# Two borrowed PSUM banks for the second pair behind a head, and its ScalarE work behind the first pair's third sum

## The chip, the cores and the metric

The kernel runs on one core of a Trainium2 chip. The core has TensorE (PE, the matmuls, with its weight loads PEld), VectorE (DVE), ScalarE (ACT), GpSimd (POOL) and SyncE (SP, which issues the loads). They run side by side and wait for each other by semaphores; each takes its own instructions in the order in which they stand. Matmuls write to PSUM; the other memory is SBUF. The metric is the device time of one execution in microseconds, the median of three runs: 1868.45 us (1867.77 to 1869.39).

## The reference

A two-layer encoder works on a prompt of 256 tokens and a sample of 512, in float32. Each layer has a mixer (an mLSTM in layer 0, windowed attention in layer 1) and a feed-forward part, each behind an RMS norm with a modulation and a residual. The change touches the feed-forward part alone:

```python
def conv_ffn(h, w_up, conv_w, conv_b, w_down):
    u = h @ w_up
    u = lax.conv_general_dilated(u, conv_w[:, None, :], window_strides=(1,),
                                 padding=((CONV_WIDTH // 2, CONV_WIDTH // 2),),
                                 dimension_numbers=('NWC', 'WIO', 'NWC'),
                                 feature_group_count=2 * D_FF) + conv_b
    g = u[..., :D_FF]
    val = u[..., D_FF:]
    return (jax.nn.silu(g) * val) @ w_down
```

The width of the model is 1024, that of g and of val 2816 each, and the conv has three taps.

## The kernel before

The two sequences stand side by side as 768 columns, features on the 128 partitions. A float32 product is made of three matmuls: a value is split into a high part (`whi`, a ScalarE CAST, line 236) and the rest (`wlo`, a DVE subtraction, line 237), and high x high, high x low and low x high are summed in PSUM.

The up projection runs in 11 rounds p; round p makes 256 features of g and 256 of val. Each is one *pair* (i = 0 and 1): two rows of 128 features. A pair isn't multiplied out directly. The 2x2 blocks of weights and activations are combined first, so that seven block products do instead of eight. The combined activations (`T1` to `T4`, `B11`, `B21`, `B22`, held as `zh`/`zl`, `yh`/`yl` and `bq`) are made once per layer; the combined weights are made for each pair from two loads of 512 KB (`raw`) by four POOL instructions (lines 1158, 1161, 1162, 1170), then split. One block product is 12 matmuls of 384 columns (lines 1125, 1126, 1128).

Round 0 is the *head*: its order on PE, ACT and DVE is written out by hand, and it also does, for round 1, the products with B11 and B21. So the two pairs of round 1 have `rest` set and five products each, which `pair` puts into banks e, b and d: T1 into e; T2 into b, which begins as a copy of what the head left (line 1174); then d begins as a copy of b (line 1185), and T3 is added to it, the *third sum*, which ScalarE copies out as u3 (line 1196); B22 is added to b; T4 is added to d, the *fourth sum*. DVE makes two rows from b plus e's copy (lines 1179, 1198) and from e plus u3 (line 1199); ScalarE evicts r2 (line 1138).

There are eight PSUM banks. Four are fixed in this part (`bank(0)` to `bank(3)`, named ps in the profile); four rotate (`pa`), and the down projection takes one of them for each of its tiles. A row that is done goes through the conv (ACT line 1356, DVE taps in lines 1358 and 1359), silu (1366), POOL's product of g and val (1371) and its split (236, 237); then `down` multiplies and DVE adds the residual (563).

Apart from the head a scheduler sets the order within each engine, from its own estimate of times. `issue_after(x)` holds instructions behind x on x's engine; `behind` are two instructions of the head. A *mark* is a matmul whose result is not used: it opens a bank for sums that don't begin with a fresh product, since the copy writes over it.

Of the kernel before, what the change touches and what calls it, by code (L numbers as in the profile page):

```python
# [25 lines left out]
H = T // 2  # L26
# [52 lines left out]
def col(t):  # L79

    return t + (GAP if t >= 256 else 0)
# [64 lines left out]
class Net:  # L146
# [1003 lines left out]
    def pair(self, pool, u, bank, rows, rest=False, behind=None):  # L1150


        nc = self.nc
        r1, r2 = rows
        rb, ra = (self.load(u, h) for h in (1, 0))
        q = [t[:, 512 * i : 512 * (i + 1)] for t in (ra, rb) for i in range(2)]
        tt = nc.gpsimd.tensor_tensor
        tt(q[2], q[2], q[3], ALU.add)
        if not rest:
            wa = self.split(ra)  # L1160
        tt(q[0], q[2], q[0], ALU.subtract)  # L1161
        tt(q[1], q[1], q[0], ALU.subtract)
        s1h, s1l = (pool.tile([P, 512], R, tag=t, name=self.nm(t), bufs=1) for t in ("s1h", "s1l"))
        part = lambda w, i: [t[:, 512 * i : 512 * (i + 1)] for t in w]
        fork = r1[:, col(H) :]
        if not rest:
            fork = a = bank(0)
            self.quarters(a, part(wa, 0), self.B11, True)
        self.fp_copy_split(s1h, s1l, q[2])
        tt(q[2], q[3], q[0], ALU.subtract)  # L1170
        wc = self.split(ra)
        wb = self.split(rb)
        e, b = bank(1), bank(2)
        nc.scalar.copy(b, fork)
        p5 = self.tmp([P, H])

        def fifth():
            self.quarters(e, (s1h, s1l), self.T1, True)
            nc.scalar.copy(p5, e)

        if not rest:
            fifth()
        self.quarters(b, part(wc, 0), self.T2, False)
        d = bank(3)
        fork = nc.scalar.copy(d, b)
        if behind:
            with self.tc.issue_after(fork.ins):
                behind()
        if rest:
            fifth()  # L1190
        else:
            self.quarters(a, part(wa, 1), self.B21, False)
            self.evict(r1, a)
        self.quarters(d, part(wb, 0), self.T3, False)
        u3 = self.tmp([P, H])
        nc.scalar.copy(u3, d)  # L1196
        self.quarters(b, part(wc, 1), self.B22, False)
        nc.vector.tensor_tensor(r1[:, col(H) :], b, p5, ALU.add)  # L1198
        nc.vector.tensor_tensor(r2[:, col(H) :], e, u3, ALU.add)
        self.quarters(d, part(wb, 1), self.T4, False)  # L1200
        self.evict(r2, d)

    def prepare(self, u0, l):

        flat = [z.rearrange("p j k t -> p (j k t)") for z in (self.zh, self.zl)]
        place = lambda j: [z[:, j : j + 1024] for z in flat]

        ahead = [place(12 * H), place(4 * H)]
        wa = place(0)
        spare = None  # L1210
        if l:

            spare = self.slab([P, 3072], R)
            wa = [spare[:, 1024 * (z + 1) : 1024 * (z + 2)] for z in range(2)]
        self.fp_copy_split(*wa, self.load(u0 + 1, 0))
        for i in range(0 if l else 2):
            self.fp_copy_split(*ahead[i], self.load(u0 + 3 + i, 0))
        return wa, ahead, spare
# [122 lines left out]
    def ffn(self, l, xt, pool, last_tile, apply, keep=None):  # L1341
        nc = self.nc
        u0 = U_FFN + l * NPART * 3
        early = self.prepare(u0, l)
        next(last_tile)

        urows = [self.slab([P, 4, TG]) for _ in range(2)]
        for urow in urows:
            nc.gpsimd.memset(urow[:, :, 256 : 256 + GAP], 0.0)

        behind = []

        def conv(u, y, ch):
            cb = self.cst(CB + l * 44 + ch)
            w = lambda tap: self.cst(CW + (l * 44 + ch) * 3 + tap)
            nc.scalar.activation(y, u, AF.Identity, bias=cb, scale=w(1))  # L1356
            stt = nc.vector.scalar_tensor_tensor
            stt(y[:, 1:], u[:, :-1], w(0), y[:, 1:], ALU.mult, ALU.add)  # L1358
            stt(y[:, :-1], u[:, 1:], w(2), y[:, :-1], ALU.mult, ALU.add)  # L1359


        held = []

        def silu(yrow):
            for j in range(2):
                nc.scalar.activation(yrow[:, j], yrow[:, j], AF.Silu)

        def product(yrow, g):
            for j in range(2):
                y = yrow[:, 2 + j]  # L1370
                nc.gpsimd.tensor_tensor(y, y, yrow[:, j], ALU.mult)  # L1371
                self.fp_copy_split(g[:, 0, j], g[:, 1, j], y)

        def up(p):
            urow = urows[0] if p == 0 else urows[1]
            fixed = lambda i: self.bank[i][:, :H]
            if p == 0:
                eng = mybir.EngineType
                self.ready(HALVES[0])
                with self.tc.manual_schedule(engines={eng.PE, eng.Activation, eng.DVE}):  # L1380
                    behind[:] = self.head(u0, last_tile, pool, urows, mark, early)
            yrow = self.slab([P, 4, TG])
            g = self.slab([P, 2, 2, TG], R)
            for i in range(2):
                if p:
                    rows = [urow[:, 2 * i + j] for j in range(2)]
                    with ExitStack() as order:
                        for ins in behind[2 * i :] if p == 1 else ():
                            order.enter_context(self.tc.issue_after(ins))

                        other = p == i == 1
                        bank = lambda j: self.pa()[:, :H] if j == 1 and other else fixed(j)
                        self.pair(pool, u0 + 3 * p + i, bank, rows, p == 1, held.pop() if held else None)
                for j in range(2):
                    conv(urow[:, 2 * i + j], yrow[:, 2 * i + j], i * FC + 2 * p + j)
                if i == 0:
                    held.append(lambda: silu(yrow))
            if p:
                product(yrow, g)
            else:  # L1400
                gate = held.pop()
                held.append(lambda: (gate(), product(yrow, g)))
            return g

        def mark(t):

            hi, _ = self.quarter(self.B11)
            self.mm(t, hi[0][:, :P], hi[0], True, True)

        def down(p, g):  # L1410
            ws = (w for _, w in self.halves(u0 + 3 * p + 2))
            chunk = lambda w, i: [t[:, 512 * i : 512 * (i + 1)] for t in w]

            def tile(w, c, rng):
                s0, s1, _ = rng
                o = self.pa()[:, : s1 - s0]
                cs = slice(c % 4 * P, (c % 4 + 1) * P)
                for i in range(2):
                    wh, wl = chunk(w, i)
                    gh, gl = (g[:, z, i, col(s0) : col(s0) + s1 - s0] for z in range(2))  # L1420
                    self.mm(o, wh[:, cs], gh, i == 0, False)
                    self.mm(o, wh[:, cs], gl, False, False)
                    self.mm(o, wl[:, cs], gh, False, i == 1)
                self.resid(xt, o, l, 40, c, rng)

            if p < NPART - 1:
                for h, w in enumerate(ws):
                    for rng in SAMPLE, PROMPT:
                        for c in range(4 * h, 4 * h + 4):
                            tile(w, c, rng)  # L1430
                return
            ws = list(ws)
            for rng in RANGES:
                norm = Norm(self, xt, rng, apply, last=keep is None and rng is RANGES[-1], adds=None if keep is not None else nc.vector)
                for c in range(KC):
                    tile(ws[c // 4], c, rng)
                    norm.square(c)
                    if keep is not None or rng is not RANGES[-1] or c < 3:
                        self.tick(0.65)
                if keep is not None:  # L1440
                    self.save_x(xt, keep, rng)
                self.start(rng, norm.stages())

        prev = None
        for p in range(NPART):
            g = up(p)
            if prev is not None:
                down(*prev)
            prev = (p, g)
        down(*prev)  # L1450
# [180 lines left out]
```

## Time and profile before

| what | value |
|---|---|
| median of three runs | 1868.45 us |
| profiled execution | 1867.75 us, span 1865.8 us |
| TensorE granted clock, mean | 0.990 |
| PE busy, whole span | 1801.3 us of 1865.8 |
| DVE / ACT / POOL busy | 1393.3 / 903.8 / 488.1 us |
| round 1's pairs, layer 0 and layer 1 | from about 560 and from about 1366 us |

In a row of the profile stand line, engine, operation and tiles (written <- read). A wait is put down to what ended it last. A timeline row gives start and duration in us; an instruction's duration has a tail in which the next one has begun. Waits of PE cost time only where PE has no other work in its order, and PE takes its matmuls in order.

### The profile page before, as it was taken

Reading aid. Unit: us, or ns where it says so; the run is one execution under the profiler, and the core shown is the slowest. Engines: PE = TensorE matmul, PEld = TensorE weight load, DVE = VectorE, ACT = ScalarE, POOL = GpSimd, SP = SyncE. Lnnn points to the kernel's source line nnn. Section 1 sums busy time; section 2 is a strip of 40 time slices with the busy share of each in tenths; the row PEclk is TensorE's granted clock in tenths of the full one; section 3 lists DMA queues with packets and bytes.
Section 4 is the critical chain, followed back from the end, with each engine's and each line's share of the span. In section 5 each row is a group of like instructions: output and inputs, shape, how many; then the busy total and the mean of one; then the engine's idle time right before and its main releaser. Section 6 shows DMA issues by size and latency. Waiting matters only on the chain. (4 is left out here: it accounts for less than half of the span.)

```text
span 1865.8 us, 29038 instructions
## 1 busy us (share of the span) xinstructions
PE 1801.3 (97%) x11270; PEld 1660.2 (89%) x11270; DVE 1393.3 (75%) x2296; ACT 903.8 (48%) x1832; POOL 488.1 (26%) x387
## 2 busy tenths in 40 slices
PE   6999999999999999999999999989999999999997
PEld 3988877888998999999999898879989999999996
DVE  4765676876689877777777768875998778777877
ACT  4444434344456444444444556763575444444443
POOL 1101001022024333333331313330134333333322
PEclk9999999999999999999999999999999999999998
DMA  8343546536312212222222321212222222222212
GB/s 328 119 151 120 181 159 226 191 109 209 114 40 79 80 59 69 70 70 72 69 70 82 102 91 41 86 59 91 80 80 80 68 68 69 68 68 68 68 35 68
DMA packets 64245, 184.48 MB, mean 99 GB/s; under 512 B 6167, under 2 KB 23831, under 8 KB 64108
## 3 DMA queue, kind: packets, MB, share of 16 engines
q1 hardware_dynamic: 64108, 182.63, 29.5%
q8 instruction: 88, 1.44, 0.3%
q14 instruction: 49, 0.40, 0.1%
HBM read 176.17 MB, written 6.43 MB: 98 GB/s over the span
## 5 line engine op out<-in xcount | busy, mean ns | idle before, releaser
L236 ACT CAST whi<-raw 128x1024 fp32r<-128x1024 f32 x237 | 248.4, 1048 | 368.7 <-PE pa L230 162.6
L237 DVE TENSOR_TENSOR wlo<-raw,whi 128x1024 fp32r<-128x1024 f32 x237 | 321.4, 1356 | 113.0 <-ACT whi L236 111.4
L230 PE MATMUL pa<-slab,whi 128*128 128x256 f32 (+1 forms) x1472 | 347.1, 332 | 3.3 <-DVE slab L563 3.3
L230 PEld LDWEIGHTS pa<-slab,whi 128*128 128x128 f32 x1472 | 254.0, 189 | 27.6 <-DVE slab L563 4.8
L563 DVE SCALAR_TENSOR_TENSOR slab<-pa,mod,slab 128x256 f32<-128x256 f32 (+1 forms) x368 | 211.6, 593 | 72.7 <-PE pa L230 72.3
L230 PE MATMUL ps<-zh,whi 128*128 128x256 f32 (+2 forms) x688 | 232.4, 339 | 6.5 <-ACT whi L236 5.2
L230 PE MATMUL pa<-slab,wlo 128*128 128x256 f32 (+1 forms) x736 | 234.5, 330 | 0.0
L230 PE MATMUL ps<-zh,wlo 128*128 128x256 f32 (+2 forms) x688 | 227.3, 333 | 2.6 <-DVE wlo L237 2.6
L230 PE MATMUL ps<-zl,whi 128*128 128x256 f32 (+2 forms) x688 | 227.5, 333 | 0.4 <-DVE zl L526 0.4
L1125 PE MATMUL ps<-zh,whi 128*128 128x384 f32 x504 | 172.3, 342 | 3.7 <-ACT nt L1196 1.9
L1126 PE MATMUL ps<-zl,whi 128*128 128x384 f32 x504 | 169.9, 337 | 0.8 <-DVE zl L1082 0.8
L1128 PE MATMUL ps<-zh,wlo 128*128 128x384 f32 x504 | 169.0, 335 | 0.0
L230 PEld LDWEIGHTS pa<-slab,wlo 128*128 128x128 f32 x736 | 139.3, 189 | 13.0 <-DVE wlo L237 0.4
L230 PEld LDWEIGHTS ps<-zh,whi 128*128 128x128 f32 x688 | 131.8, 192 | 18.8 <-ACT whi L236 6.3
L230 PEld LDWEIGHTS ps<-zh,wlo 128*128 128x128 f32 x688 | 131.5, 191 | 13.3 <-DVE wlo L237 3.6
L230 PEld LDWEIGHTS ps<-zl,whi 128*128 128x128 f32 x688 | 131.9, 192 | 9.5 <-DVE zl L526 0.8
L1161 POOL TENSOR_TENSOR raw<-raw,raw 128x512 f32<-128x512 f32 x40 | 52.0, 1301 | 320.0 <-DVE wlo L237 246.4
L1371 POOL TENSOR_TENSOR slab<-slab 128x772 f32<-128x772 f32 x44 | 86.4, 1965 | 169.4 <-DVE slab L1359 157.5
L1358 DVE SCALAR_TENSOR_TENSOR slab<-slab,cstt,slab 128x771 f32<-128x771 f32 x88 | 107.6, 1225 | 26.5 <-ACT slab L1356 26.4
L482 DVE SCALAR_TENSOR_TENSOR ada<-raw,silc,ada 128x1024 f32<-128x1024 f32 x84 | 106.7, 1306 | 11.0 <-DMA raw<-in_adaln_w_dram 11.0
L1359 DVE SCALAR_TENSOR_TENSOR slab<-slab,cstt,slab 128x771 f32<-128x771 f32 x88 | 110.7, 1258 | 0.8
L1356 ACT ACTIVATE slab<-slab,cstt 128x772 f32<-128x772 f32 x88 | 91.0, 1034 | 39.1 <-DVE slab L1198 36.1
(301 smaller groups left out, 4130.6 us busy)
## 6 DMA issues: line engine op xcount, KB each, us to landing
raw<-in_w_dram SPq DMA_DIRECT2D x208, 512.0 KB, 3.7
raw<-in_adaln_w_dram SPq DMA_DIRECT2D x84, 512.0 KB, 4.6
slab<-in_x_dram SPq DMA_DIRECT2D x12, 512.0 KB, 7.5
slab<-in_adaln_w_dram SPq DMA_DIRECT2D x12, 512.0 KB, 10.2
slab<-mrows SPq DMA_DIRECT2D x8, 384.0 KB, 6.2
xs<-slab SPq DMA_DIRECT2D x6, 512.0 KB, 3.1
bt<-brow SPq DMA_DIRECT2D x16, 192.0 KB, 3.1
slab<-xs SPq DMA_DIRECT2D x6, 512.0 KB, 6.0
```

The lines of the kernel that those rows point to most:

```text
L230: self.nc.tensor.matmul(out, lhsT, rhs, start=start, stop=stop)
L236: nc.scalar.copy(hi, src)
L237: return nc.vector.tensor_tensor(lo, src, hi.bitcast(F32), ALU.subtract)
L482: stt(acc[:, s], row, w, acc[:, s], ALU.mult, ALU.add)
L563: self.nc.vector.scalar_tensor_tensor(x, o, self.mod[l][:, gc + c, q : q + 1], x, ALU.mult, ALU.add)
L1125: mm(o, wh[:, k], hi[k], start=start and k == 0, stop=False, skip_group_check=True)
L1126: mm(o, wh[:, k], lo[k], start=False, stop=False, skip_group_check=True)
L1128: mm(o, wl[:, k], hi[k], start=False, stop=k == 3, skip_group_check=True)
L1356: nc.scalar.activation(y, u, AF.Identity, bias=cb, scale=w(1))
L1358: stt(y[:, 1:], u[:, :-1], w(0), y[:, 1:], ALU.mult, ALU.add)
L1359: stt(y[:, :-1], u[:, 1:], w(2), y[:, :-1], ALU.mult, ALU.add)
L1371: nc.gpsimd.tensor_tensor(y, y, yrow[:, j], ALU.mult)
```

## The change

Before, of the second pair of round 1 only e lay in a rotating bank. Now e and b do, both asked for ahead of the pair, and b's bank is opened by a mark. And `pair` returns the copy of its third sum; the second pair's instructions on ScalarE are held behind the first pair's copy. Lines from 1202 on are one higher after the change, those behind the new block in `up` five higher.

```diff
         u3 = self.tmp([P, H])
-        nc.scalar.copy(u3, d)
+        last = nc.scalar.copy(u3, d)
         self.quarters(b, part(wc, 1), self.B22, False)
...
         self.evict(r2, d)
+        return last.ins
...
                         for ins in behind[2 * i :] if p == 1 else ():
                             order.enter_context(self.tc.issue_after(ins))
-
-                        other = p == i == 1
-                        bank = lambda j: self.pa()[:, :H] if j == 1 and other else fixed(j)
-                        self.pair(pool, u0 + 3 * p + i, bank, rows, p == 1, held.pop() if held else None)
+                        bank = fixed
+                        if p == i == 1:
+
+                            others = {j: self.pa()[:, :H] for j in (1, 2)}
+                            mark(others[2])
+                            bank = lambda j: others.get(j) or fixed(j)
+                            order.enter_context(self.tc.issue_after(last))
+                        last = self.pair(pool, u0 + 3 * p + i, bank, rows, p == 1, held.pop() if held else None)
```

The order of the instructions moves at three places that matter, the same in both layers. First ScalarE, around the copy of the first pair's third sum. In the names, `nt_5647` is u3, `slab_5563` the conv's row with its silu, `whi_5695` and `whi_5699` the second pair's weights before, `s1h_5693` and `whi_5698` after. Before:

```order
L236 CAST whi_5695<-raw_5685 128x1024
L1138 COPY slab_5136<-pa_5385 128x128
L1138 COPY slab_5136<-pa_5385 128x256
L236 CAST slab_5564<-slab_5563 128x772
L1356 ACTIVATE slab_5563<-slab_5136,cstt 128x772
L1366 ACTIVATE slab_5563<-slab_5563 128x772
L236 CAST whi_5699<-raw_5683 128x1024
L1196 COPY nt_5647<-ps_4536 128x384
L1174 COPY ps_4535<-slab_5137 128x384
```

After:

```order
L1357 ACTIVATE slab_5563<-slab_5136,cstt 128x772
L236 CAST slab_5564<-slab_5563 128x772
L1367 ACTIVATE slab_5563<-slab_5563 128x772
L1196 COPY nt_5647<-ps_4536 128x384
L236 CAST s1h_5693<-raw_5686 128x512
L236 CAST whi_5698<-raw_5688 128x1024
L1174 COPY pa_5684<-slab_5137 128x384
```

The two CASTs ahead of the copy are gone from there, the second pair's casts now follow it, and the copy that begins the second pair's b goes into a rotating bank.

Then PE, where the first pair's fourth sum (`ps_4536`) and the second pair's T1 (`pa_5703` before, `pa_5683` after) meet. Before:

```order
L1125 MATMUL pa_5703<-zh,s1h_5690 128x384
L1126 MATMUL pa_5703<-zl,s1h_5690 128x384
L1128 MATMUL pa_5703<-zh,s1l_5691 128x384
L1125 MATMUL ps_4536<-zh,whi_5595 128x384
L1126 MATMUL ps_4536<-zl,whi_5595 128x384
L1128 MATMUL ps_4536<-zh,wlo_5596 128x384
```

After:

```order
L1125 MATMUL ps_4536<-zh,whi_5595 128x384
L1126 MATMUL ps_4536<-zl,whi_5595 128x384
L1128 MATMUL ps_4536<-zh,wlo_5596 128x384
L1125 MATMUL pa_5683<-zh,s1h_5693 128x384
L1126 MATMUL pa_5683<-zl,s1h_5693 128x384
L1128 MATMUL pa_5683<-zh,s1l_5694 128x384
```

T1 of the second pair stood between the third and the fourth sum; now it stands behind the fourth.

Last DVE, from the last tap of the first pair's second row on. Before (`s1l_5942` belongs to the third pair):

```order
L1198 TENSOR_TENSOR slab_5137<-ps_4535,nt_5600 128x384
L237 TENSOR_TENSOR wlo_5700<-raw_5683,whi_5699 128x1024
L1359 SCALAR_TENSOR_TENSOR slab_5563<-slab_5136,cstt,slab_5563 128x771
L1199 TENSOR_TENSOR slab_5137<-ps_4534,nt_5647 128x384
L237 TENSOR_TENSOR s1l_5942<-raw_5930,s1h_5941 128x512
```

After (`s1l_5694` and `wlo_5699` belong to the second pair, `wlo_5703` to its third sum):

```order
L1198 TENSOR_TENSOR slab_5137<-ps_4535,nt_5600 128x384
L237 TENSOR_TENSOR slab_5564<-slab_5563,slab_5564 128x772
L1360 SCALAR_TENSOR_TENSOR slab_5563<-slab_5136,cstt,slab_5563 128x771
L1199 TENSOR_TENSOR slab_5137<-ps_4534,nt_5647 128x384
L237 TENSOR_TENSOR s1l_5694<-raw_5686,s1h_5693 128x512
L237 TENSOR_TENSOR wlo_5699<-raw_5688,whi_5698 128x1024
L1359 SCALAR_TENSOR_TENSOR slab_5577<-slab_5137,cstt,slab_5577 128x771
L1360 SCALAR_TENSOR_TENSOR slab_5577<-slab_5137,cstt,slab_5577 128x771
L237 TENSOR_TENSOR slab_5564<-slab_5563,slab_5564 128x772
L1359 SCALAR_TENSOR_TENSOR slab_5577<-slab_5137,cstt,slab_5577 128x771
L237 TENSOR_TENSOR wlo_5703<-raw_5686,whi_5702 128x1024
```

The s1l behind that tap and L1199 is now the second pair's, and four conv and split instructions stand between its T2 weights and those of its third sum.

## The prediction

> **What bounds the kernel now.** First the page's head: TensorE's share says whether time can be won anywhere else.
>
> ```profile
> span 1865.8 us, 29038 instructions
> PE 1801.3 (97%) x11270; PEld 1660.2 (89%) x11270; DVE 1393.3 (75%) x2296; ACT 903.8 (48%) x1832; POOL 488.1 (26%) x387
> ```
>
> TensorE (PE) is idle for 65 us of 1865.8, and the change leaves its matmuls as they are but for two marks. So the change is worth what it does to PE's waits. Next, the table of waits of PE over the whole span (total, times, longest):
>
> ```profile
> PE ps L1128 <- DVE s1l L237: 2.8, 2, 1.4
> PE ps L1125 <- ACT nt L1196: 1.9, 2, 0.9
> PE ps L1125 <- ACT ps L1174: 1.4, 2, 0.7
> PE ps L1126 <- DVE bq L1107: 0.4, 2, 0.2
> PE pa L230 <- DVE slab L563: 3.3, 6, 0.7
> ```
>
> The first three come twice each, once behind the head of each layer, which is where the change is. Their places are in PE's timeline (start, duration; in brackets the idle time and who ended it):
>
> ```profile
> 567.39 0.34 PE L1125 MATMUL pa<-zh,s1h 128*128 128x384 f32 x1
> 567.58 0.34 PE L1126 MATMUL pa<-zl,s1h 128*128 128x384 f32 x1
> ...
> 573.55 0.34 PE L1128 MATMUL pa<-zh,s1l 128*128 128x384 f32 x1
> 574.81 0.44 PE L1125 MATMUL ps<-zh,whi 128*128 128x384 f32 x1 [0.93 <-ACT nt L1196]
> ...
> 576.84 0.34 PE L1128 MATMUL ps<-zh,wlo 128*128 128x384 f32 x1
> 577.88 0.44 PE L1125 MATMUL ps<-zh,whi 128*128 128x384 f32 x1 [0.70 <-ACT ps L1174]
> ...
> 580.25 0.34 PE L1126 MATMUL ps<-zl,s1h 128*128 128x384 f32 x1
> 581.97 0.45 PE L1128 MATMUL ps<-zh,s1l 128*128 128x384 f32 x1 [1.38 <-DVE s1l L237]
> ```
>
> In a run without waits a 384-column matmul starts 0.175 us after the one before, and the first after a wait loses 0.10 more. So the stops cost 1.26-0.18+0.10 = 1.18, 1.04-0.18+0.10 = 0.96 and 1.72-0.18+0.10 = 1.64: 3.78 us a layer, 7.6 in all. Behind this place little is left to win:
>
> ```profile
> 567.00:584.00 17.00, 13.99 (x77) 12.98 (x76) 16.96 (x14) 12.36 (x20) 10.47 (x5) 1.00 0.30 94
> 592.00:680.00 88.00, 87.80 (x505) 83.69 (x504) 68.55 (x79) 42.18 (x66) 32.95 (x20) 1.00 0.20 66
> ```
>
> In these stages (PE, PEld, DVE, ACT, POOL busy) PE is full from 592 on, so what is lost or won at 567 to 592 stays. In the stops themselves the full engine is VectorE (DVE), 16.96 of 17.00 us. Why it is full stands in its timeline beside GpSimd's (POOL):
>
> ```profile
> 568.40 2.50 POOL L1371 TENSOR_TENSOR slab<-slab 128x772 f32<-128x772 f32 x1 [5.97 <-ACT slab L1366]
> 570.87 2.01 POOL L1170 TENSOR_TENSOR raw<-raw,raw 128x512 f32<-128x512 f32 x1
> 579.52 1.84 POOL L1371 TENSOR_TENSOR slab<-slab 128x772 f32<-128x772 f32 x1 [4.43 <-DVE slab L1359]
> ```
>
> ```profile
> 566.43 1.21 DVE L237 TENSOR_TENSOR wlo<-raw,whi 128x1024 fp32r<-128x1024 f32 x1
> 567.57 0.68 DVE L237 TENSOR_TENSOR s1l<-raw,s1h 128x512 fp32r<-128x512 f32 x1
> 568.17 1.01 DVE L1358 SCALAR_TENSOR_TENSOR slab<-slab,cstt,slab 128x771 f32<-128x771 f32 x1
> 569.22 2.51 DVE L1359 SCALAR_TENSOR_TENSOR slab<-slab,cstt,slab 128x771 f32<-128x771 f32 x1
> 571.65 2.31 DVE L237 TENSOR_TENSOR wlo<-raw,whi 128x1024 fp32r<-128x1024 f32 x1
> 579.30 0.54 DVE L1199 TENSOR_TENSOR slab<-ps,nt 128x384 f32<-128x384 f32 x1
> 579.77 2.14 DVE L237 TENSOR_TENSOR s1l<-raw,s1h 128x512 fp32r<-128x512 f32 x1
> 585.93 0.95 DVE L237 TENSOR_TENSOR slab<-slab,slab 128x772 fp32r<-128x772 f32 x1
> ```
>
> DVE's instructions with two inputs in SBUF and POOL's take turns: the s1l split takes 0.68 at 567.57 and 2.14 at 579.77, where POOL's product began 0.25 earlier; the tap takes 1.01 at 568.17 and 2.51 at 569.22; the wlo split 1.21 and 2.31. A product thus holds DVE off for about 1.7, a POOL sum of 512 columns for 2.31-1.21 = 1.10. L1199, which reads one input from PSUM, takes its 0.54 beside a product.
>
> The Trainium skill, page "SBUF — State Buffer", section "Who interferes with whom", says the same as a rule: a VectorE instruction with two SBUF inputs and a GpSimd instruction that reads SBUF share a port pair, and whichever starts second waits for the other's whole instruction. By that rule the third stop would come back at whichever s1l follows the product; by the solo row, 0.68, it would not. The 2.14 agrees with the rule. With it the sum below is +3.4 us; with the solo rows it would be -4.2.
>
> **The change, part by part.** The second pair's work on ScalarE now stands behind the first pair's copy of its third sum (L1196), and its sums e and b lie in two banks of the other pool, so PE's order changes: third sum, fourth sum of the first pair with nothing between, then T1 and T2 of the second. I follow it through layer 0, by hand, with these rows (consecutive starts on DVE and ACT are 0.06 to 0.10 less than the durations: the wlo split occupies 1.14, a tap 0.93, the slab split 0.87, s1l 0.60).
>
> ```profile
> 567.47 0.85 ACT L1366 ACTIVATE slab<-slab 128x772 f32<-128x772 f32 x1
> 570.94 0.84 ACT L236 CAST slab<-slab 128x772 fp32r<-128x772 f32 x1 [1.25 <-POOL slab L1371]
> 573.36 1.03 ACT L236 CAST whi<-raw 128x1024 fp32r<-128x1024 f32 x1
> 574.29 0.47 ACT L1196 COPY nt<-ps 128x384 f32<-128x384 f32 x1
> ...
> 577.76 0.62 ACT L236 CAST s1h<-raw 128x512 fp32r<-128x512 f32 x1
> ```
>
> A load of half a weight unit takes, from issue to landing, among the loads of 550 to 600:
>
> ```profile
> DMA to landing us min/median/max: 3.5/3.6/3.7
> ```
>
> Removed: the three stops, -3.78. Added:
>
> *Stop A, third to fourth sum.* From 567.39 PE does 24 matmuls, 4.2 us, to 571.6. On DVE the s1l of 567.57 is gone, so wlo (to 567.57) is followed by a tap to 568.50. POOL's product, wanted from 568.2 (silu 567.3 to 568.15), holds to 570.13; the next tap ends at 571.06. The second silu waits for that tap: 571.2 to 571.95; the copy stands behind it: to 572.43. PE goes on at 572.47: 0.87+0.10 = 0.97. The floor, with ScalarE free, is one copy and two hand-overs, about 0.8; the whi CAST, 1.03 in the row above, is no longer ahead of it.
>
> *Stop B, s1l of the second pair.* Fourth sum to 574.57, two matmuls to 574.92. DVE from 571.06: tap 0.93; POOL's sum L1158 for the third pair, whose weights are asked for when wlo ends (567.6) and land 3.6 later, gets in for 1.10 (L1198, from PSUM, beside it); slab split 0.87; tap 0.93, to 574.9. That tap releases the second product, which holds 1.8 with its hand-over while L1199 runs: 576.7. Then s1l 0.60, 577.38 with its tail. PE resumes at 577.42: 2.50+0.10 = 2.60. If the split won against the product it would be ready at 576.05, 1.25; if POOL's sum got in one tap earlier, 3.05. I take 2.60, since the same sequence (tap, product, L1199, s1l) stands at 579.30 to 579.77 above.
>
> *Stop C, first weights of the down projection.* 22 matmuls, 3.95 with the restart, to 581.37. POOL's L1170 waits for s1l, then for the wlo split (to 578.45), and ends at 579.7; two CASTs at 0.95 follow on ScalarE: 581.75. 0.42+0.10 = 0.52; between 0 and 1.0, as a CAST more or less stands ahead.
>
> *Stop D, wlo of the second pair's third sum.* PE reaches it at 583.52. DVE after 578.45: L1170's 1.10, three taps and a slab split 3.66, wlo 1.14: 584.35, PE 584.47: 0.95+0.10 = 1.05. ScalarE's copy L1185 that starts this third sum (done at 583.08) is just in time.
>
> Sum 0.97+2.60+0.52+1.05 = 5.14 against 3.78: **+1.35 a layer**. Through stop D the end is set by DVE's row (571.06 plus 13.3 us, 3.3 of it POOL's two sums and part of the product), so a smaller B only makes C and D larger.
>
> *Third pair.* Its third sum now follows T2's last matmul after four others, and the copy L1185 between them stands behind a CAST. Where such a copy is late today it costs this:
>
> ```profile
> 674.15 0.34 PE L1128 MATMUL ps<-yh,wlo 128*128 128x384 f32 x1
> 674.69 0.45 PE L1125 MATMUL ps<-zh,whi 128*128 128x384 f32 x1 [0.20 <-ACT ps L1185]
> ```
>
> 0.54-0.18 = 0.36; bounds 0 and 0.46. I take 0.35 a layer.
>
> *Marks.* One more matmul per layer ahead of 548, 0.18 each; it is hidden by the wait for L1107 there (0.2 idle each time in the table), and costs 0.18 if that cover goes.
>
> *Banks.* The down projection has two fewer banks until the second pair's last adds are done (588 to 589 by this reckoning); PE wants its third bank at 594. Nothing.
>
> *Ripples.* The norms after layer 0 and the attention are ordered a little differently. PE idles 3.9 and 6.8 us there:
>
> ```profile
> 1000.00:1062.00 62.00, 58.10 (x403) 54.49 (x403) 48.95 (x91) 28.75 (x57) 20.16 (x20) 0.97 0.35 112
> 1198.00:1262.00 64.00, 57.17 (x457) 48.70 (x456) 48.84 (x205) 45.46 (x145) 20.94 (x39) 0.95 0.21 65
> ```
>
> No step there is added; I take 0, with 1.5 either way.
>
> Two layers: 2 x (1.35+0.35) = **+3.4 us**. The profiled execution took 1867.75, its span and 1.95 around it; the median is 0.70 above, and I add the sum to the median: 1871.9.
>
> **The rivals.** *Faster: DVE and POOL don't meet.* If stop B's s1l and D's wlo ran at their solo lengths (0.68, 1.21), only A and half of C are left, about 1.7 a layer against 3.78: -4.2, 1864.3. It decides if DVE's row ends about 2 us before 584.35 or more. For it: ScalarE gets to the copy earlier and loses the CAST ahead of it. Against it: 2.14 and 2.31 in the rows above.
>
> *The stops only change places.* New ones of 3.8 a layer, no third-pair wait: 1868.4. For it: the removed and added stops are alike in kind. It needs POOL's sum L1158 to fall wholly beside an instruction from PSUM, and stop C to vanish.
>
> *Slower: DVE stays behind into the down projection.* Then residual adds (L563) come late and PE finds its four banks unread, up to 0.7 a time by the wait table. Two or three more such waits a layer are 2.8 to 4.2 in all: 1874.7 to 1876. It decides if DVE is more than about 4 us later than I have it at 588. For it: DVE's 16.96 of 17.00. Against it: 68.55 of 88.00 just behind.
>
> **How the numbers follow.** About 0.2% (3.7 us) is what a measurement of this kernel tells from no change: 1864.7 to 1872.2. The forecast, 1871.9 (its own range 1870.0 to 1873.5), has 0.45 and lies across that bound: 0.25 within, 0.20 beyond. Stops that change places 0.13, DVE behind 0.30, no meeting 0.12. So faster 0.12, same 0.38, slower 0.50. From 1866.5 to 1876.0 leaves out nearly all of the faster case and a tail above, under 2 in 10.
>
> **What would show it.** The waits for L1174 and the first L1196 gone or moved: the fourth sum right behind the third with about 0.7 idle for L1196; an s1l wait of 2 to 2.5 us five to six us earlier than now, the split itself over 2 us long beside a product; shorter new waits for a whi CAST and a wlo split at 581 to 585; PE past the second pair's B22 at 588.4. An s1l of 0.68 there, or PE past it before 586, makes me wrong towards faster; waits for L563 after 594, towards slower.

## The result

The changed kernel takes 1872.09 us in the median of 13 executions (1867.3 to 1875.34), the kernel before 1868.11 in 13 executions beside them (1866.13 to 1870.7). The ratio is 1.0022, with a 95% interval of 1.0014 to 1.003: slower by about 4 us.

Its profiled execution has a span of 1872.7 us. Of the 6.9 us by which that is longer than the span shown of before, 3.3 were there already at 560 us, ahead of the place of the change: the first conv instruction of ScalarE in layer 0 stands at 561.96 instead of 558.65. So the two traces are compared by place. That distance, 3.31 ahead of the place, is 5.42 behind it (the same instructions at 756.06 and 761.48), 4.38 ahead of layer 1's, and 6.8 behind that: 2.1 and 2.4 us a layer, less 1.0 us in the attention between them, where no step was changed (the account of the prediction below shows that this 1.0 is not the change's).

The head of the page and the table of PE's waits of the changed kernel:

```profile
span 1872.7 us, 29033 instructions
PE 1806.8 (96%) x11272; PEld 1663.7 (89%) x11272; DVE 1392.0 (74%) x2296; ACT 904.5 (48%) x1832; POOL 485.4 (26%) x387
```

```profile
PE pa L1128 <- DVE s1l L237: 4.7, 2, 2.4
PE pa L230 <- DVE slab L563: 3.8, 8, 0.6
PE ps L1125 <- ACT nt L1196: 1.3, 2, 0.7
...
PE ps L1125 <- ACT ps L1185: 0.4, 2, 0.2
```

The wait for L1174 is gone, that for L1196 is shorter, that for s1l has grown from 1.4 to 2.4 each (before the change PE waited for the third pair's s1l, now for the second pair's), and two waits for L563 have come. PE's timeline of layer 0, from the end of the first pair's third sum to the second pair's:

```profile
574.73 0.34 PE L1128 MATMUL ps<-zh,wlo 128*128 128x384 f32 x1
575.72 0.44 PE L1125 MATMUL ps<-zh,whi 128*128 128x384 f32 x1 [0.65 <-ACT nt L1196]
...
578.11 0.34 PE L1126 MATMUL pa<-zl,s1h 128*128 128x384 f32 x1
580.82 0.45 PE L1128 MATMUL pa<-zh,s1l 128*128 128x384 f32 x1 [2.37 <-DVE s1l L237]
...
582.60 0.53 PE L1128 MATMUL pa<-zh,s1l 128*128 128x384 f32 x1
582.92 0.53 PE L1125 MATMUL pa<-zh,whi 128*128 128x384 f32 x1
...
585.80 0.34 PE L1125 MATMUL pa<-zh,whi 128*128 128x384 f32 x1
...
587.78 0.34 PE L1126 MATMUL ps<-zl,whi 128*128 128x384 f32 x1
587.95 0.39 PE L1128 MATMUL ps<-zh,wlo 128*128 128x384 f32 x1
```

Stop A is 0.99-0.18+0.10 = 0.91, stop B 2.71-0.18+0.10 = 2.63. Stops C and D are not there. In their place ten matmuls from 582.60 to 585.80 stand 0.32 apart instead of 0.176: 3.20 us for 1.76 us of work, 1.44 lost. The windows show why (the seventh number is the granted clock):

```profile
582.00:586.00 4.00, 4.00 (x16) 4.00 (x15) 3.96 (x4) 2.91 (x5) 1.04 (x1) 0.57 0.43 124
1388.00:1392.00 4.00, 3.81 (x14) 3.81 (x15) 3.96 (x4) 2.95 (x4) 2.19 (x1) 0.58 0.20 32
```

Half speed for some 3 us, in both layers. Before, this stretch ran at 1.00:

```profile
582.00:586.00 4.00, 4.00 (x20) 3.51 (x21) 4.00 (x4) 2.54 (x4) 1.94 (x1) 1.00 0.00 0
```

DVE and POOL meet as they did before, only earlier in PE's work:

```profile
577.25 1.01 DVE L1360 SCALAR_TENSOR_TENSOR slab<-slab,cstt,slab 128x771 f32<-128x771 f32 x1
578.18 0.55 DVE L1199 TENSOR_TENSOR slab<-ps,nt 128x384 f32<-128x384 f32 x1
578.64 2.12 DVE L237 TENSOR_TENSOR s1l<-raw,s1h 128x512 fp32r<-128x512 f32 x1
...
586.63 2.35 DVE L237 TENSOR_TENSOR wlo<-raw,whi 128x1024 fp32r<-128x1024 f32 x2
```

```profile
578.40 1.81 POOL L1372 TENSOR_TENSOR slab<-slab 128x772 f32<-128x772 f32 x1 [1.89 <-DVE slab L1360]
```

Further on, the down projection waits for a residual add, once a layer (607.21, and 0.55 idle at 1414.79), and the third pair for L1185 (the wait that was at 674.69 is gone):

```profile
607.21 0.73 PE L230 MATMUL pa<-slab,whi 128*128 128x512 f32 x2 [0.35 <-DVE slab L563]
618.85 0.44 PE L1125 MATMUL ps<-zh,whi 128*128 128x384 f32 x1 [0.18 <-ACT ps L1185]
```

### The profile page after: what moved, and what is told of

Read it like the earlier page. It is cut to its first block, busy times and chain, and to the rows that moved or that the text cites. A ratio compares the mean times of both kernels' runs of the same rounds, so it can differ in the third digit from the quotient of the medians.

```text
span 1872.7 us, 29033 instructions
## 1 busy us (share of the span) xinstructions
PE 1806.8 (96%) x11272; PEld 1663.7 (89%) x11272; DVE 1392.0 (74%) x2296; ACT 904.5 (48%) x1832; POOL 485.4 (26%) x387
## 3 DMA queue, kind: packets, MB, share of 16 engines
q8 instruction: 88, 1.44, 0.3%
## 4 chain that ended last, share of the span: by engine, by line
PE 78%; DVE 10%; issue 5%; DMA 3%; ACT 2%; POOL 1%; SPq 0%; POOLq 0%; DVEq 0%; ACTq 0%
PE ps L230 24%; PE pa L230 23%; PE ps L1125 10%; PE ps L1126 9%; PE ps L1128 9%; DVE wlo L237 1%; DMA raw<-in_w_dram 1%; DMA bt<-brow 1%; PE pa L965 1%; DVE slab L1359 1%; DMA raw<-in_adaln_w_dram 1%; DVE slab L563 1%; DVE slab L1360 1%; DVE t L941 1%; ACT whi L236 1%
## 5 line engine op out<-in xcount | busy, mean ns | idle before, releaser
L237 DVE TENSOR_TENSOR wlo<-raw,whi 128x1024 fp32r<-128x1024 f32 x237 | 316.2, 1335 | 118.5 <-ACT whi L236 115.6
L230 PE MATMUL pa<-slab,whi 128*128 128x256 f32 (+1 forms) x1472 | 346.7, 332 | 3.8 <-DVE slab L563 3.8
L230 PEld LDWEIGHTS pa<-slab,whi 128*128 128x128 f32 x1472 | 254.1, 189 | 28.3 <-DVE slab L563 5.9
L563 DVE SCALAR_TENSOR_TENSOR slab<-pa,mod,slab 128x256 f32<-128x256 f32 (+1 forms) x368 | 212.3, 593 | 75.6 <-PE pa L230 75.2
L230 PE MATMUL ps<-zh,whi 128*128 128x256 f32 (+2 forms) x688 | 233.3, 340 | 6.3 <-ACT whi L236 4.9
L230 PE MATMUL pa<-slab,wlo 128*128 128x256 f32 (+1 forms) x736 | 234.2, 330 | 0.0
L230 PE MATMUL ps<-zh,wlo 128*128 128x256 f32 (+2 forms) x688 | 227.7, 334 | 2.3 <-DVE wlo L237 2.3
L230 PE MATMUL ps<-zl,whi 128*128 128x256 f32 (+2 forms) x688 | 228.7, 334 | 0.7 <-DVE zl L526 0.7
L230 PEld LDWEIGHTS pa<-slab,wlo 128*128 128x128 f32 x736 | 139.3, 189 | 12.9
L230 PEld LDWEIGHTS ps<-zh,whi 128*128 128x128 f32 x688 | 132.6, 193 | 18.9 <-ACT whi L236 6.0
L230 PEld LDWEIGHTS ps<-zh,wlo 128*128 128x128 f32 x688 | 131.8, 192 | 12.8 <-DVE wlo L237 3.1
L230 PEld LDWEIGHTS ps<-zl,whi 128*128 128x128 f32 x688 | 132.6, 193 | 10.1 <-DVE zl L526 1.1
L1372 POOL TENSOR_TENSOR slab<-slab 128x772 f32<-128x772 f32 x44 | 82.2, 1869 | 166.7 <-DVE slab L1360 153.9
L1158 POOL TENSOR_TENSOR raw<-raw 128x512 f32<-128x512 f32 x40 | 65.6, 1640 | 187.7 <-DMA raw<-in_w_dram 170.8
```

The costliest lines, as they stand in the source:

```text
L230: self.nc.tensor.matmul(out, lhsT, rhs, start=start, stop=stop)
L237: return nc.vector.tensor_tensor(lo, src, hi.bitcast(F32), ALU.subtract)
L563: self.nc.vector.scalar_tensor_tensor(x, o, self.mod[l][:, gc + c, q : q + 1], x, ALU.mult, ALU.add)
```

## The experiments

Two readings of this stand against each other. *Theory*: DVE's row of instructions, with POOL's turns in it, sets when the stretch ends; the half clock only fills time in which PE would have waited at C and D. *Rival*: the half clock, 1.44 us a layer, is the loss, and without it the change would be about even. A second rival: the loan of the banks, or ScalarE's order, costs by itself. All ratios are to the kernel before, run beside each on the same chip.

| kernel | ratio | 95% interval |
|---|---|---|
| the change | 1.0022 | 1.0014 to 1.003 |
| the change again | 1.0021 | 1.0009 to 1.0032 |
| only the banks | 1.0020 | 1.0011 to 1.003 |
| only the order | 1.0028 | 1.0019 to 1.0038 |
| 12 unused matmuls | 1.0023 | 1.0014 to 1.0032 |
| product on DVE | 0.9999 | 0.9988 to 1.001 |
| early s1 split | 1.0048 | 1.003 to 1.0065 |
| early s1 split, product on DVE | 1.0015 | 1.0006 to 1.0023 |
| only the banks, product on DVE | 1.0001 | 0.999 to 1.0011 |
| before, product on DVE | 1.0001 | 0.9988 to 1.0015 |
| before, product on DVE, again | 0.9992 | 0.9982 to 1.0001 |

**One half of the change at a time.** Only the banks, without the hold behind L1196:

```diff
-                            order.enter_context(self.tc.issue_after(last))
```

> Only the two banks; the hold behind the copy of the third sum (L1196) is left out, so T1 and T2 of the second pair may stand between the first pair's third and fourth sum. Theory (the end of the stretch is set by DVE's and POOL's turns): PE then has 22 matmuls to do where it stopped 0.9 and 0.6 us in the trace of before, so those two stops go (-2.1 us a layer), but it arrives that much earlier at the s1l split behind the second POOL product, and the wait there grows from 1.4 to between 3 and 4 us: the stretch ends within 0.5 us a layer of before, 1867 to 1870. If the clock falls to half behind that longer stop, as it did in the trace of after, up to 1.4 us a layer more, 1871. Rival (banks and ScalarE's order are what cost or win): the s1l wait stays at 1.4, the two stops are won outright, -2.1 us a layer, 1864.

Only the hold, with the second pair's b in its fixed bank as before the change:

```diff
-                            others = {j: self.pa()[:, :H] for j in (1, 2)}
-                            mark(others[2])
+                            others = {1: self.pa()[:, :H]}
```

> Only the hold behind L1196; the second pair's b stays in its fixed bank, as before the change. Theory: PE's waits as in the trace of after (about 0.7 for L1196, 2.3 to 2.4 for s1l, a half clock behind it), span within 1 us of after, ratio to before 1.0015 to 1.0025; the banks alone cost nothing, unless the waits for the down projection's residual adds (L563, 0.4 and 0.6 in after) go with them, which would be -0.9 in all. Rival (the loan of a bank is what costs): the L563 waits go and the time is that of before.

Measured: 1873.05 with the banks, 1875.25 with the order, 1868.89 before. Each half alone costs about what both together cost, so they don't add up. With the banks alone, PE's timeline has this:

```profile
580.30 0.42 PE L1125 MATMUL ps<-zh,s1h 128*128 128x384 f32 x1 [1.91 <-DVE slab L1199]
580.56 0.34 PE L1126 MATMUL ps<-zl,s1h 128*128 128x384 f32 x1
582.26 0.46 PE L1128 MATMUL ps<-zh,s1l 128*128 128x384 f32 x1 [1.36 <-DVE s1l L237]
```

The stops for L1196 and L1174 are gone, PE has its 22 matmuls early, and then stands, in the third pair's T1, for 1.91 + 1.36 = 3.3 us: the wait foreseen for s1l, shared with L1199, which stands just ahead of it on DVE and frees the bank. Behind it the clock falls to 0.57 here too:

```profile
582.00:586.00 4.00, 3.74 (x12) 3.65 (x13) 3.96 (x5) 3.97 (x7) 1.69 (x1) 0.57 0.00 0
```

The 2.1 us a layer that the two stops had cost were not won. With the order alone PE waits 0.65 and 2.37 as in the changed kernel, and the waits for L563 (0.34 and 1.31) did not go. So the loss needs neither the loan nor the mark, and with the banks alone it does not need the hold: either half brings PE to DVE's late splits. The ratio with the order alone, 1.0028, lies a little above theory's 1.0015 to 1.0025: here PE comes to the wlo matmul of the third sum at 585.62 without a wait, 0.6 us after that split was done on DVE (583.83 plus 1.21), so a part of the half clock is paid there.

**Work for PE in the stop.** 12, then 4 unused matmuls into the rotating bank of e behind the first pair's fourth sum, so that PE stops for less or hardly at all (in the code the pair also returns its last matmul):

```diff
+                            with self.tc.issue_after(last[1]):
+                                for _ in range(12):
+                                    mark(others[1])
```

> The changed kernel with 12 unused matmuls of 384 columns (the opening matmul of a bank, whose result is written over) added in each layer behind the first pair's fourth sum, so that PE works through most of the wait for the s1l split: 12 times 0.176 is 2.1 of its 2.4 us. Nothing else moves. Theory (DVE's row sets the end): the idle time falls to about 0.3, the clock stays at 1.00 at 582 to 586, and the waits that the half clock covered come out: about 0.5 for the whi CAST ahead of the first down weights and up to 1.0 for the wlo split of the second pair's third sum; the stretch ends within 0.4 us a layer of after, 1871 to 1872.5. Rival (the half clock is what makes the change slower): those waits stay away, each layer wins 1.4 us, 1869.

> The changed kernel with 4 unused matmuls a layer behind the first pair's fourth sum instead of 12, 0.7 us of work: the stop for s1l is about 1.7 idle. If the length of the stop is what halves the clock, it stays at 1.00 here as in the kernel before behind a stop of 1.4, and the waits for the whi CAST and the wlo split of the third sum are back (1.5 to 2 us together). The time from the third sum of the first pair to the first wlo matmul of the second pair's third sum is 13.2 us as with 0 and with 12 extra matmuls, since DVE's row sets it.

> The changed kernel once more, beside the next two on one chip. The s1l stop of 2.4 comes in both layers again; if the half clock behind it is set by the stop, it comes in both layers again too (0.57 to 0.58 of 4 us); if it was a chance of that execution, it is missing in one or both, and waits for a whi CAST (about 0.4) and a wlo split (about 1.4) are there instead. The ratio to before is 1.0014 to 1.003 either way.

With 12 matmuls, PE's timeline and the windows:

```profile
573.33 0.34 PE L1128 MATMUL ps<-zh,wlo 128*128 128x384 f32 x1
574.34 0.44 PE L1125 MATMUL ps<-zh,whi 128*128 128x384 f32 x1 [0.67 <-ACT nt L1196]
...
579.47 0.44 PE L1128 MATMUL pa<-zh,s1l 128*128 128x384 f32 x1 [0.32 <-DVE s1l L237]
...
583.24 0.33 PE L1128 MATMUL pa<-zh,s1l 128*128 128x384 f32 x1
583.78 0.51 PE L230 MATMUL pa<-slab,whi 128*128 128x512 f32 x1 [0.21 <-ACT whi L236]
...
584.99 0.34 PE L1126 MATMUL ps<-zl,whi 128*128 128x384 f32 x1
586.58 0.44 PE L1128 MATMUL ps<-zh,wlo 128*128 128x384 f32 x1 [1.25 <-DVE wlo L237]
```

```profile
582.00:586.00 4.00, 3.12 (x16) 2.31 (x14) 3.96 (x5) 3.77 (x6) 0.00 (x0) 1.00 0.42 133
1388.00:1392.00 4.00, 4.00 (x25) 4.00 (x24) 3.96 (x4) 2.94 (x4) 2.21 (x1) 1.00 0.19 40
```

With 4:

```profile
571.13 0.34 PE L1128 MATMUL ps<-zh,wlo 128*128 128x384 f32 x1
...
577.23 0.44 PE L1128 MATMUL pa<-zh,s1l 128*128 128x384 f32 x1 [1.67 <-DVE s1l L237]
...
581.55 0.50 PE L230 MATMUL pa<-slab,whi 128*128 128x512 f32 x1 [0.20 <-ACT whi L236]
...
584.33 0.45 PE L1128 MATMUL ps<-zh,wlo 128*128 128x384 f32 x1 [0.89 <-DVE wlo L237]
```

The clock stays at 1.00, and stops C and D come out of hiding: 0.46 and 1.51 us with 12 (by 583.24 to 583.78 and 584.99 to 586.58, less 0.18, plus 0.10), 0.46 and 1.14 with 4. The end does not move. From the last matmul of the first pair's third sum to the first wlo matmul of the second pair's, in layer 0:

| kernel | us |
|---|---|
| the change: 574.73 to 587.95 | 13.22 |
| the change again: 572.59 to 585.83 | 13.24 |
| 4 matmuls: 571.13 to 584.33 | 13.20 |
| 12 matmuls: 573.33 to 586.58 | 13.25 |
| product on DVE: 571.79 to 583.08 | 11.29 |

Full clock or half, the same 13.2 us, and 1.0023 beside 1.0022 in the time. In layer 1 it is 13.18, 13.22 and 13.20, but 12.26 with 12 matmuls: there PE had lost 0.96 ahead of the stretch (a wait at 1366.42) and so had that much less to wait, while DVE's row from L1198 to the split took 11.41, against 11.35 in layer 0 of the change. The rival falls: in the changed kernel the half clock costs next to nothing, since PE would have stood still instead. The run of the change again has the half clock in both layers, so it came four times in four with this order. The single time with 4 matmuls, 1874.06, tells nothing more by itself.

**The turns of DVE and POOL.** The product of round 0, which is made between the parts of round 1's pairs, on DVE:

```diff
-        def product(yrow, g):
+        def product(yrow, g, eng=nc.gpsimd):
...
-                nc.gpsimd.tensor_tensor(y, y, yrow[:, j], ALU.mult)
+                eng.tensor_tensor(y, y, yrow[:, j], ALU.mult)
...
-                held.append(lambda: (gate(), product(yrow, g)))
+                held.append(lambda: (gate(), product(yrow, g, nc.vector)))
```

> The changed kernel, with one edit: the product of round 0 that the pairs of round 1 run between their parts is made on DVE instead of POOL, so that POOL's product no longer holds DVE off. Theory: stop A stays at 0.7 to 0.9; the s1l split takes 0.6 to 0.7 instead of 2.1 and the wait for it falls from 2.4 to about 0.5; small waits for wlo splits (0.3 to 1.1) may appear behind it; the clock stays at 1.00 in 582 to 586. That is 2 to 3 us of stops a layer, 2.2 less than after measured: 1867 to 1868. Rival one (DVE is simply full, the turns don't matter): moving two products of about 0.8 us onto DVE makes the waits longer, over 1873. Rival two (the half clock is the whole loss): no stop over 2 us, so the loss is gone, 1868, but with the s1l split still about 2 us long.

DVE's timeline, then PE's:

```profile
575.37 0.68 DVE L237 TENSOR_TENSOR s1l<-raw,s1h 128x512 fp32r<-128x512 f32 x1
575.97 0.95 DVE L1372 TENSOR_TENSOR slab<-slab 128x772 f32<-128x772 f32 x1
576.84 2.31 DVE L237 TENSOR_TENSOR wlo<-raw,whi 128x1024 fp32r<-128x1024 f32 x1
```

```profile
571.79 0.34 PE L1128 MATMUL ps<-zh,wlo 128*128 128x384 f32 x1
572.70 0.45 PE L1125 MATMUL ps<-zh,whi 128*128 128x384 f32 x1 [0.57 <-ACT nt L1196]
576.10 0.44 PE L1128 MATMUL pa<-zh,s1l 128*128 128x384 f32 x1 [0.69 <-DVE s1l L237]
579.21 0.44 PE L1128 MATMUL pa<-zh,wlo 128*128 128x384 f32 x1 [0.73 <-DVE wlo L237]
...
583.08 0.45 PE L1128 MATMUL ps<-zh,wlo 128*128 128x384 f32 x1
```

DVE has more to do by two instructions of 0.95, and its row is 13.2-11.29 = 1.9 us shorter. The s1l split takes 0.68; the wlo split behind still takes 2.31, beside POOL's L1170. The loss is gone: 1868.56 beside 1868.89 (the execution profiled here was the slowest of the twelve, 1874.96, so only the stretch is compared). Theory's 1867 to 1868 was a little low. So the loss needs POOL's products in DVE's way. They are in its way before the change too (2.51 and 2.14 in the prediction's rows), and the same edit may win some 2 us there (below), so the change may still be behind by that much when neither kernel has them; these runs can't tell. The Trainium skill's rule in "SBUF — State Buffer", "Who interferes with whom", which the prediction weighed, agrees with each of these durations.

**The s1 split ahead of the product.** Only what follows the s1 split of the second pair is held (`pair` takes `after`, the copy L1196):

```diff
+            if after:
+                order.enter_context(self.tc.issue_after(after))
             wc = self.split(ra)
```

> The changed kernel with one edit: of the second pair only what follows its s1 split is held behind the copy L1196, so s1h and s1l are made as early as before the change and don't meet the second product. Theory: the stop of 2.4 for s1l goes, but DVE's row is as long as ever, so the wlo split of T2 becomes late instead (up to 3.4, since 12 more matmuls are 2.1 us of work in front of it but L1170 and two wlo splits stand on the row), and the layer ends within 0.5 us of after: ratio 1.0015 to 1.0025. Rival (the place of the s1l split behind the product is what costs): 1.5 to 2.4 us a layer are won, ratio 0.9995 to 1.0005.

> Both edits at once: the early s1 split and the product of round 0 on DVE. Theory: the row is 1.8 us shorter than in the run with the early split alone, as it was for the changed kernel, so 3 to 3.6 us less in all: ratio 0.9995 to 1.0005, the stops again under 1 us each. Rival (order matters once the turns are gone): below before by as much as the kernel before gains from that product, ratio 0.998 to 0.999.

PE's timeline of the first of the two in both layers, DVE's in layer 0, and the windows behind the stops:

```profile
579.42 0.69 PE L1128 MATMUL pa<-zh,wlo 128*128 128x384 f32 x1 [3.40 <-DVE wlo L237]
...
587.11 0.33 PE L1125 MATMUL ps<-zh,whi 128*128 128x384 f32 x1
...
1390.85 0.45 PE L1128 MATMUL pa<-zh,wlo 128*128 128x384 f32 x1 [2.46 <-DVE wlo L237]
```

```profile
577.19 3.32 DVE L237 TENSOR_TENSOR wlo<-raw,whi 128x1024 fp32r<-128x1024 f32 x2
```

```profile
579.60:585.60 6.00, 6.00 (x19) 6.00 (x20) 6.00 (x7) 3.59 (x6) 0.74 (x1) 0.50 0.55 175
1391.40:1394.40 3.00, 3.00 (x11) 3.00 (x11) 3.00 (x5) 2.15 (x5) 0.00 (x0) 0.50 0.76 253
```

The wait moved from s1l to wlo as foreseen, to 3.40 in layer 0, but the time is 1.0048, beyond theory's 1.0025. Here DVE had both wlo splits done by 580.5, long before PE came to the third sum at 587.11, so PE set the end itself, and by this reading, which no run of its own tests, the half clock was paid in full: in layer 0 it lasted 6 us, with 19 matmuls that need 3.3 us at full speed. That is 2.7 us, and about 1.1 in layer 1. So theory holds for the changed kernel, and not for every order of this stretch: the half clock is free only while DVE is late anyway. With the product on DVE as well the waits fall to 1.32 us and less, the clock stays, and the ratio is 1.0015, 0.0033 less, where theory had the end at 1.0000; a wait of 0.84 for a whi CAST, once a layer in both, remains, and what else keeps it above is open.

**Something better than before?** The same product on DVE in the kernel before, twice, and with the banks alone; the edit is the one above.

> The kernel before with that one edit: the product of round 0 on DVE instead of POOL. Theory (DVE's row and POOL's turns set the end): the two turns go (a tap of 2.51 and an s1l of 2.14 become about 1.0 and 0.7, and two products of 0.95 come in), which in the changed kernel shortened DVE's row by 1.8 us a layer; so the s1l stop of 1.64 goes, the other two stay within 0.3 us, and the time is 1.2 to 1.8 us a layer below before: 1865 to 1866.5 (ratio 0.998 to 0.9987). Rival (DVE is full, whoever makes the product): no gain, ratio 0.9995 to 1.0005, with another wait where the s1l stop was.

> The kernel before with the product of round 0 on DVE, once more: its first 12 executions had a median of 1866.25 beside 1868.59 of before, but three at 1873.5 to 1877.6, so that their mean ratio was 1.0001 (0.9988 to 1.0015). If those three were chance, the ratio is now 0.9985 to 0.9993 with an interval that excludes 1. If something in this kernel halves the clock now and then, some executions are 5 us and more above the others again and the ratio stays at about 1.

> Only the two banks, no hold behind L1196, and the product of round 0 on DVE. Theory: the two waits behind 22 early matmuls (1.9 for L1199 and 1.4 for s1l with the banks alone) fall by 1.8 in sum, the clock stays at 1.00, so 1.8 plus about 1.2 us a layer less than with the banks alone (1.0020): ratio 0.9985 to 0.9995. If the loan of the banks pays once the turns are gone, it ends below the kernel before with the same product; if DVE's row still sets the end, level with it or above.

In the kernel before, the stops for L1196 and s1l go, that for L1174 grows, and one for L1185 in the third pair comes:

```profile
577.78 0.44 PE L1125 MATMUL ps<-zh,whi 128*128 128x384 f32 x1 [1.13 <-ACT ps L1174]
...
612.68 0.44 PE L1125 MATMUL ps<-zh,whi 128*128 128x384 f32 x1 [0.89 <-ACT ps L1185]
```

The medians are 1866.25 beside 1868.59 and 1866.87 beside 1869.05, 2.3 and 2.2 us less, but three of the first twelve executions took 1873.5 to 1877.6, and both intervals hold 1. A gain of some 2 us is likely and not shown. The banks with the product on DVE give 1868.1 beside 1868.59, a ratio of 1.0001 where theory had 0.9985 to 0.9995: PE's waits for L1199 fell to 0.81 and the half clock is gone, yet the loan won nothing that these runs can tell. No version here is shown to beat the kernel before.

## Why the prediction was right

It forecast 1871.9; the median is 1872.09. Point by point, for layer 0:

- *Removed*, 3.78 us: all three stops are gone from their places.
- *Stop A*: 0.97 forecast, 0.91 measured.
- *Stop B*: 2.60 forecast, 2.63 measured, from the sequence tap, product, L1199, s1l that was read off the trace before; the s1l split takes 2.12. The runs with the product on DVE show its cause.
- *Stops C and D*, 0.52 and 1.05: absent, and 1.44 of half clock in their place. The forecast had no clock in it. It came out right because both are different ways for PE to arrive when DVE is ready. The step that carried the sum was "Through stop D the end is set by DVE's row": its own count came to 13.05 us from third sum to wlo matmul (571.42 to 584.47), and 13.2 were measured, with the half clock and with the full one. With 4 matmuls in the stop, C and D measured 0.46 and 1.14.
- *Third pair*, 0.35: the wait came (the matmul ahead starts at 618.34: 0.51-0.18 = 0.33), but the one at 674.69, 0.36, went in the same layer. The term should have been zero.
- *Not forecast*: one wait for L563 a layer, 0.35 idle in layer 0 and 0.55 in layer 1 (0.34 and none when the change was run again). It is the mild form of the rival in which DVE stays behind into the down projection; that rival's 2.8 us and more did not come.
- *Ripples*, 0 with 1.5 either way: -1.0 in the attention, from the distances of the two traces. It belongs to the execution and not to the order: in the one of before the clock was at half there (0.51 in 1248 to 1250), and 32 matmuls of L230 took 3.62 us from 1248.03, which take 1.97 in the changed kernel (from 1253.79), and 1.97 as well in both profiled executions of the kernel before with the product on DVE.
- *The mark by which it was to be judged*: PE past the second pair's B22 at 588.4, with the 3.31 by which this execution was late already 591.7; it was past at 591.87.

The sum of 1.70 a layer stands against 2.1 and 2.4 in the trace, of which 0.5 or so a layer has no place in these rows. With the -1.0 between the layers the trace has 3.5 in all, beside a forecast of 3.4: that the terms which were off (the third pair, L563, the attention) cancel is luck. The mechanism of the sum, stops A and B and DVE's row, was right by itself.

## What to carry to other kernels

A stop of the full engine is worth taking away only if what it waits for then comes earlier. Here VectorE's row set the end, so reordering TensorE's work moved the stop to the next thing that this row makes, while a change that shortened the row (a product on VectorE for 0.95 us, where GpSimd's had held it off for 1.4 to 1.5 and released later work as late) took the loss away at once. To tell what sets the end, fill the stop with unused work: if the end stays, the stop was only the place where the lateness showed.

## What the runs showed of the hardware

TensorE's granted clock fell to half, for about 3 us or twice that, behind some of PE's stops. In this stretch it fell behind stops of 2.36 to 2.38 us idle (six times in six: the change twice and the order alone, two layers each), of 2.46 and 3.40, and of 1.91 and 1.36 close together (twice in two); it did not behind 1.67 and 1.68, nor behind 1.38 in the kernel before. The fall comes up to 1.7 us after PE has begun to work again (580.82 and 582.5 in layer 0 of the change), and at half speed a matmul of 384 columns starts every 0.32 us instead of 0.176.

These numbers give no bound, since equal stops end differently. Each of the 13 executions profiled also stops once for 2.38 to 2.40 us in the attention (at 1228 to 1237): behind that the clock fell in eleven and stayed at 1.00 in two, one of them the changed kernel's first (1235.07). Behind a stop of 2.02 or 2.03 at 306 to 310 it fell in six of 13. And in the kernel before it fell to half behind stops of 1.41 and 1.44 that lie about 1 us apart (409.18 and 411.58). A fall that comes in one execution and not in another moves its time, by 1.65 us where 32 matmuls of L230 took 3.62 instead of 1.97 (1248.03 in the kernel before), and so is a part of the spread between executions.

The Trainium skill, page "TensorE: Matmul & The Clock Gate", Part 1, has the clock halved after an idle window of some 3.4 us, and full again after a busy one, in windows that run freely beside the work. The half rate agrees with the trace, and the length of the slow part comes near (3.2 us in layer 0 of the change). By that rule a stop of 2.37 us is too short to halve it; here such a stop did so six times, and the measurement decides. That equal stops end differently would fit windows that run freely, but no run here shows where a window begins.
